# Newton results kept in PSUM, and the first norm and first weights prepared without GpSimd

## The chip, the cores and the metric

The kernel runs on one core of a Trainium2 chip. The time is device time in microseconds (us) of one launch. Before the change it is 2960.99 us, the median of three runs (2956.82 to 2964.68). The profile is of one further execution, which took 2968.41 us.

Names: PE is TensorE's matmul queue, PEld its weight loads, DVE is VectorE, ACT is ScalarE, POOL is GpSimd, SP is SyncE, which issues all DMAs here.

## The reference, cut to what matters

The kernel computes one layer of a hybrid encoder for 1280 tokens (1024 and 256) of width 1024: an RMS norm, one wide input projection, three mixers (latent attention, a bidirectional RWKV-7 scan, cross-attention to memory tokens), gates, an output projection, and a gated convolution MLP. The change touches the first part alone, the projections and the norms in them:

```python
h = rms_norm(x, norm_mix_g);  proj = h @ w_in            # c_q, c_kv, k_r, rw, xq, gates
q = rms_norm(rms_norm(c_q, q_norm_g) @ w_uq, mla_qn_g)   # per head of 96, then rope
k = rms_norm(concat(rms_norm(c_kv) @ w_ukv, k_r), mla_kn_g)
kk = k7 * k_k;  kk = kk / max(sqrt(sum(kk * kk)), 1e-12) # per head of 64
m = rms_norm(mem) @ w_mkv;  xqh = rms_norm(xq, x_qn_g);  mk = rms_norm(mk, x_kn_g)
```

Every `rms_norm` over channels is a sum of squares and one over its root.

## The kernel before, in words

Activations stand transposed: channels on the 128 partitions, tokens along the row, in three chunks of 512, 512 and 256 tokens (`CH`). Every matmul is done in three passes, because each fp32 operand is split into a high part `h` and a rest `l` (`split`, line 123: the copy that rounds on ACT or DVE, and the subtraction on POOL or DVE); the passes are lines 133, 134 and 135 in `mm3`.

The norm of the input is not applied before the projection. `norm1` (line 392) loads a chunk of x, multiplies by the gain and splits it into `hh` and `hl` (`scaled_split`, lines 284 and 285), sums the squares of its eight channel tiles into `nacc` (`mean_sq`, lines 272 to 279, where squares and additions take turns on ACT, DVE and POOL), and leaves a generator, `norm1_stats`, that splits `nacc`, sums it over the partitions with two matmuls against ones (`col_sum`, line 239, into a PSUM tile `nst` with the tag `tr`), and makes one over the root. That is `rsq`: on ACT the logarithm, the exponential and its square (lines 251 to 253), then on DVE one step of Newton in two instructions (lines 256 and 257). The result, `rbc`, is scaled once more (line 263), and every projection is multiplied by it when it leaves PSUM, as in line 424 for `xq` and 879 for the gates; a q head leaves through lines 679 and 680.

Four PSUM banks with the tag `mm` hold projections, four with the tag `tr` hold the small sums and transposes. A projection's bank comes free when DVE or ACT has read it.

Order of the work. `xq_proj` (line 436) comes first: it loads the weights `wqf` in eight pieces and splits them (line 446), and goes through chunk 0 channel tile by channel tile for all four heads at once, so that PE can start when the first tile is there. In that loop, at `k == 6`, `drain` runs what is left of the norm, `col_sum` included, so that its two matmuls stand in PE's queue between tiles 5 and 6. All four `mm` banks are then full, and chunk 1 can't start before line 424 has emptied one. Chunks 1 and 2 follow, then the memory's projection, gates, latents, q heads (`q_out`), keys (`k_out`), values and the RWKV tiles (`rw_out`), interleaved by generators. Weights of 128 columns come through `w4_load` (line 315), two tiles in flight, in the order of `w4_order`; `xq_proj` calls it once ahead of chunks 1 and 2.

The order on each engine's queue is fixed at compile time: a planner takes the instructions by priority (the order of the program, unless a block asks for high priority) as soon as its own simulated clock says that they are ready. On the chip each queue is then worked off in that order.

Of the kernel before, what the change touches and what calls it, by code (L numbers as in the profile page):

```python
# [11 lines left out]
ALU = mybir.AluOpType  # L12
# [15 lines left out]
EPS = 1e-6  # L28
# [69 lines left out]
class Kern:  # L98
# [128 lines left out]
    def parts(self, p, x, cn, K=128):  # L227

        hi = p.tile([128, 512], F32R, tag="sqh", name="sqh", bufs=2)
        lo = p.tile([128, 512], F32R, tag="sql", name="sql", bufs=2)  # L230
        self.split(x[:K, :cn], hi[:K, :cn], lo[:K, :cn])
        return hi, lo
# [14 lines left out]
    def rsq(self, y, t, tmp, scale=1.0, eps=0.0):  # L247


        nc = self.nc  # L250
# [4 lines left out]
        s, op, c = (eps / scale, ALU.add, -3.0 / scale) if eps else (-0.5 * scale, ALU.mult, 1.5)  # L255
        nc.vector.scalar_tensor_tensor(out=tmp, in0=t, scalar=s, in1=tmp, op0=op, op1=ALU.mult)
# [11 lines left out]
    def mean_sq(self, p, src, cn):  # L268
# [4 lines left out]
        for k in range(1, 8):  # L273
            sq = p.tile([128, 512], F32, tag="nsq", name="nsq", bufs=3)
            if k % 2:
# [3 lines left out]
            (nc.vector if k % 2 else nc.gpsimd).tensor_add(out=acc[:, :cn], in0=acc[:, :cn], in1=sq[:, :cn])  # L279
# [112 lines left out]
    def norm1(self, p, ci, w=None):  # L392
# [16 lines left out]
        acc = self.mean_sq(p, lambda k: x[k], cn)  # L409
# [4 lines left out]
    def norm1_stats(self, p, acc, ci):  # L414
        c0, cn = CH[ci]
        x = self.parts(p, acc, cn)
        yield
        yield from self.rsq_x(p, self.rbc1[ci], x, cn)

    def head_norm(self, p, ps, cn, rbc, gain, dst):  # L420
# [9 lines left out]
        yield from self.rsq(sq[:, :cn], self.col_sum(x, cn), tmp[:, :cn], 1.0 / 128, EPS)  # L430
        nc.vector.scalar_tensor_tensor(
            out=raw[:, :cn], in0=raw[:, :cn], scalar=gain, in1=sq[:, :cn], op0=ALU.mult, op1=ALU.mult
# [3 lines left out]
    def xq_proj(self, p):  # L436
# [4 lines left out]
        def load(k):  # L441
# [4 lines left out]
            self.split(f, wq[0][:, k, :], wq[1][:, k, :], "dve")  # L446
# [8 lines left out]
        for k in range(8):  # L455
            if k == 6:
# [12 lines left out]
        self.w4_load()  # L469
        for ci in (1, 2):  # L470
            c0, cn = CH[ci]
            for h in range(4):
# [197 lines left out]
    def q_out(self, p, ps, h, c0, cn):  # L670
# [16 lines left out]
        yield from self.rsq(sq[0:96, :cn], st[0:96], zs[0:96, :cn], EPS / 384)  # L687
        nc.vector.tensor_mul(out=z[0:96, :cn], in0=z[0:96, :cn], in1=sq[0:96, :cn])
# [34 lines left out]
    def k_out(self, p, ps, j, kro, c0, cn):  # L723
# [13 lines left out]
        yield from self.rsq(sq[:, :cn], st, tmp[:, :cn])  # L737
        nc.vector.tensor_mul(out=z[:, :cn], in0=z[:, :cn], in1=sq[:, :cn])
        i = (3 * j + c0 // 512) % 2
        for e in range(2):  # L740
            kr = self.krb[64 * e : 64 * e + 32, 512 * i : 512 * i + 512]
            (nc.vector if e else nc.gpsimd).tensor_mul(out=kr[:, :cn], in0=kro[:, cs], in1=sq[64 * e : 64 * e + 32, :cn])
# [57 lines left out]
    def rw_out(self, p, m, x, g2):  # L800
# [7 lines left out]
        elif m < 8:  # L808
# [4 lines left out]
            for c0, cn in CH:  # L813
# [8 lines left out]
                yield from self.rsq(sq[:, :cn], st, tmp[:, :cn])  # L822
                nc.vector.scalar_tensor_tensor(
                    out=kk[:, c0 : c0 + cn], in0=xc, scalar=self.vec("k_k", j), in1=sq[:, :cn],
# [1276 lines left out]
```

## Time and profile before

| | us |
|---|---|
| median of three runs | 2960.99 |
| profiled execution, its own time | 2968.41 |
| its span | 2966.6 |
| PE busy in the span | 2781.4 (94%) |
| DVE, ACT, POOL busy | 1544.2, 1173.3, 1358.5 |
| chain that ended last: share of PE | 38% |

Stages by time: `xq` up to about 92 us, memory and gates to about 120, latents and q heads to about 372, keys and values to about 516, RWKV tiles to about 640; the scan with attention as its filler to about 1950, and after that the output projection and the MLP, in which PE is busy nearly without a break. [...]

### The profile page before, as it was taken

The page shows a single profiled execution, that of the slowest core. Times are in us where ns is not written, and L with a number is a line of the kernel's source. Part 1 is how long each engine was busy: PE and PEld are TensorE (multiplying, and loading weights), DVE is VectorE, ACT ScalarE, POOL GpSimd, SP SyncE. Part 2 cuts the span into 40 slices and gives each one's busy share as a digit, 9 for nine tenths or more (in the row PEclk, how much of TensorE's full clock was granted, in tenths as well). Part 3 has the DMA queues.
Part 4 walks back from the last instruction along what each step waited for, and adds up shares of the span by engine and source line. Part 5 has one row for each costly group of instructions (what it writes and reads, how often), then busy time and mean ns, then how long its engine had stood idle before and what let it go on. Part 6 is the DMA issues. An engine that isn't in the chain of part 4 may idle for free. (4 is left out here: it accounts for less than half of the span.)

```text
span 2966.6 us, 50241 instructions
## 1 busy us (share of the span) xinstructions
PE 2781.4 (94%) x19556; PEld 2246.2 (76%) x19556; DVE 1544.2 (52%) x2576; ACT 1173.3 (40%) x2561; POOL 1358.5 (46%) x1220
## 2 busy tenths in 40 slices
PE   7998998999999999899989688999999999999999
PEld 5787787885666665477767577888888888888888
DVE  8638848566767665655565465423422323323233
ACT  5645555545555555544443234423221211212111
POOL 5546736454444344455554467743342332423323
PEclk8999999999999998899989899999999999999999
DMA  4333324553122222343343666422111111111112
GB/s 151 99 96 97 101 69 114 154 147 90 51 68 61 59 60 78 89 122 108 106 122 102 189 201 187 144 87 64 40 43 36 42 37 36 43 36 42 37 33 86
DMA packets 250005, 261.77 MB, mean 88 GB/s; under 512 B 81028, under 2 KB 178448, under 8 KB 249768
## 3 DMA queue, kind: packets, MB, share of 16 engines
q1 hardware_dynamic: 249768, 258.57, 29.6%
q8 instruction: 154, 2.52, 0.4%
q14 instruction: 83, 0.68, 0.1%
HBM read 196.64 MB, written 61.73 MB: 87 GB/s over the span
## 5 line engine op out<-in xcount | busy, mean ns | idle before, releaser
L133 PE MATMUL up<-h2h,wuh 128*128 128x512 f32 (+1 forms) x1056 | 374.2, 354 | 0.0
L134 PE MATMUL up<-h2h,wul 128*128 128x512 f32 (+1 forms) x1056 | 374.0, 354 | 0.0
L135 PE MATMUL up<-h2l,wuh 128*128 128x512 f32 (+1 forms) x1056 | 373.5, 354 | 0.0
L129 POOL TENSOR_TENSOR w4l<-w4f,w4h 128x512 fp32r<-128x512 f32 (+1 forms) x154 | 264.0, 1723 | 216.5 <-ACT w4h L126 210.4
L129 POOL TENSOR_TENSOR wul<-wuf,wuh 128x1024 fp32r<-128x1024 f32 x52 | 125.1, 2405 | 270.7 <-ACT wuh L126 270.7
L133 PEld LDWEIGHTS up<-h2h,wuh 128*128 128x128 f32 x1056 | 199.7, 189 | 28.0
L135 PEld LDWEIGHTS up<-h2l,wuh 128*128 128x128 f32 x1056 | 199.6, 189 | 27.8
L134 PEld LDWEIGHTS up<-h2h,wul 128*128 128x128 f32 x1056 | 199.7, 189 | 27.4
L1849 DVE TENSOR_TENSOR x<-x,dn 128x512 f32<-128x512 f32 (+1 forms) x192 | 113.6, 598 | 194.3 <-PE dn L135 194.3
L133 PE MATMUL proj<-hh,w4h 128*128 128x512 f32 (+1 forms) x504 | 182.2, 363 | 9.3 <-DVE go L879 5.0
L134 PE MATMUL dn<-ah,wdl 128*128 128x256 f32 (+1 forms) x528 | 187.2, 356 | 0.0
L135 PE MATMUL dn<-al,wdh 128*128 128x256 f32 (+1 forms) x528 | 184.7, 356 | 0.0
L133 PE MATMUL dn<-ah,wdh 128*128 128x256 f32 (+1 forms) x528 | 182.1, 356 | 0.4 <-ACT wdh L126 0.4
L135 PE MATMUL proj<-hl,w4h 128*128 128x512 f32 (+1 forms) x504 | 181.4, 360 | 0.0
L134 PE MATMUL proj<-hh,w4l 128*128 128x512 f32 (+1 forms) x504 | 181.0, 360 | 0.0
L126 ACT CAST w4h<-w4f 128x512 fp32r<-128x512 f32 (+1 forms) x154 | 113.2, 751 | 149.6 <-DMA w4f<-in_w_g 41.1
L133 PE MATMUL gt<-ghh,w4h 128*128 128x512 f32 x384 | 163.7, 426 | 8.3 <-ACT w4h L126 5.2
L126 ACT CAST wuh<-wuf 128x1024 fp32r<-128x1024 f32 x52 | 54.7, 1052 | 291.7 <-PE up L135 276.1
L1869 DVE TENSOR_TENSOR fraw<-up,rbc 128x512 f32<-128x512 f32 (+1 forms) x66 | 39.8, 604 | 247.7 <-PE up L135 241.0
L129 POOL TENSOR_TENSOR wdl<-wdf,wdh 128x384 fp32r<-128x384 f32 (+1 forms) x64 | 60.3, 944 | 225.1 <-ACT wdh L126 225.1
L937 DVE TENSOR_REDUCE m<-mx 128x1 f32<-128x512 f32 (+1 forms) x184 | 107.6, 601 | 105.7 <-PE mx L936 105.1
L134 PE MATMUL gt<-ghh,w4l 128*128 128x512 f32 x384 | 155.5, 405 | 7.3 <-POOL w4l L129 7.3
(392 smaller groups left out, 7418.3 us busy)
## 6 DMA issues: line engine op xcount, KB each, us to landing
w4f<-in_w_g SPq DMA_DIRECT2D x48, 512.0 KB
wuf<-in_w_up SPq DMA_DIRECT2D x44, 512.0 KB
rk<-s_rk SPq DMA_DIRECT2D x80, 192.0 KB
w4f<-in_w_g SPq DMA_DIRECT2D x48, 256.0 KB
s_gT<-go SPq DMA_DIRECT2D x40, 256.0 KB
mg<-s_gT SPq DMA_DIRECT2D x40, 256.0 KB
wdf<-in_w_down SPq DMA_DIRECT2D x48, 192.0 KB
w4f<-in_w_rw SPq DMA_DIRECT2D x30, 256.0 KB
```

What stands on the lines that cost most here:

```text
L126: nc.scalar.copy(out=hi, in_=x)
L129: (nc.gpsimd if el == "pool" else nc.vector).tensor_sub(out=lo, in0=x, in1=hi.bitcast(F32))
L133: mm(ps, lhsT=lh, rhs=rh, start=first, stop=False)
L134: mm(ps, lhsT=ll, rhs=rh, start=False, stop=False)
L135: mm(ps, lhsT=lh, rhs=rl, start=False, stop=last)
L937: nc.vector.tensor_reduce(out=m2[:, n, z : z + 1], in_=ps[:, :kn], axis=AX.X, op=ALU.max)
L1849: nc.vector.tensor_add(out=xc, in0=xc, in1=ps[:, :cn])
L1869: nc.vector.tensor_mul(out=raw[:, o : o + cn], in0=ps, in1=self.rbc[:, c0 : c0 + cn])
```

## The change

Four things change.

1. `rsq` takes an `out`. With it, both DVE instructions of the Newton step write to the bank that holds the sums, and what uses the result reads it from there. `head_norm`, `q_out`, `k_out` and the `kk` part of `rw_out` do so; the norms of x, of the memory and of the latents don't.
2. In `k_out` the rope part of the key is multiplied on DVE for both heads; before, one of the two was on POOL.
3. The first norm and the first weights: the weights `wqf` are rounded on ACT and subtracted on DVE (before: DVE and POOL); `mean_sq` for x has all squares on ACT and all additions on DVE; the split of `nacc` subtracts on DVE; that split and the whole of `rsq_x` have high priority in the planner.
4. The `drain` in chunk 0 comes at `k == 7`, and the first `w4_load` between chunks 1 and 2.

```diff
@@ -224,11 +224,11 @@
         n = x.shape[1]
         self.nc.gpsimd.tensor_tensor(out=out, in0=x, in1=self.mhalf.to_broadcast([128, n]), op=ALU.pow)
 
-    def parts(self, p, x, cn, K=128):
+    def parts(self, p, x, cn, K=128, el="pool"):
 
         hi = p.tile([128, 512], F32R, tag="sqh", name="sqh", bufs=2)
         lo = p.tile([128, 512], F32R, tag="sql", name="sql", bufs=2)
-        self.split(x[:K, :cn], hi[:K, :cn], lo[:K, :cn])
+        self.split(x[:K, :cn], hi[:K, :cn], lo[:K, :cn], "act", el)
         return hi, lo
 
     def col_sum(self, parts, cn, K=128, ones=None):
@@ -244,7 +244,7 @@
         with self.tc.issue_after(after.ins):
             self.nc.scalar.preload_act_table_set("natural_log_exp_and_others")
 
-    def rsq(self, y, t, tmp, scale=1.0, eps=0.0):
+    def rsq(self, y, t, tmp, scale=1.0, eps=0.0, out=None):
 
 
         nc = self.nc
@@ -253,6 +253,10 @@
         self.last = nc.scalar.activation(out=tmp, in_=y, func=AF.Square)
         yield
         s, op, c = (eps / scale, ALU.add, -3.0 / scale) if eps else (-0.5 * scale, ALU.mult, 1.5)
+        if out is not None:
+            nc.vector.scalar_tensor_tensor(out=out, in0=t, scalar=s, in1=tmp, op0=op, op1=ALU.mult)
+            nc.vector.scalar_tensor_tensor(out=out, in0=out, scalar=c, in1=y, op0=ALU.add, op1=ALU.mult)
+            return
         nc.vector.scalar_tensor_tensor(out=tmp, in0=t, scalar=s, in1=tmp, op0=op, op1=ALU.mult)
         nc.vector.scalar_tensor_tensor(out=y, in0=tmp, scalar=c, in1=y, op0=ALU.add, op1=ALU.mult)
 
@@ -265,18 +269,18 @@
     def small(self, p, n, tag):
         return p.tile([128, n], F32, tag=f"{tag}{n}", name=tag, bufs=2)
 
-    def mean_sq(self, p, src, cn):
+    def mean_sq(self, p, src, cn, alone=False):
 
         nc = self.nc
         acc = p.tile([128, 512], F32, tag="nacc", name="nacc", bufs=3)
         nc.scalar.activation(out=acc[:, :cn], in_=src(0), func=AF.Square)
         for k in range(1, 8):
             sq = p.tile([128, 512], F32, tag="nsq", name="nsq", bufs=3)
-            if k % 2:
+            if k % 2 or alone:
                 nc.scalar.activation(out=sq[:, :cn], in_=src(k), func=AF.Square)
             else:
                 nc.vector.tensor_mul(out=sq[:, :cn], in0=src(k), in1=src(k))
-            (nc.vector if k % 2 else nc.gpsimd).tensor_add(out=acc[:, :cn], in0=acc[:, :cn], in1=sq[:, :cn])
+            (nc.vector if k % 2 or alone else nc.gpsimd).tensor_add(out=acc[:, :cn], in0=acc[:, :cn], in1=sq[:, :cn])
         return acc
 
     def scaled_split(self, x, g, hi, lo):
@@ -406,16 +410,19 @@
                 w(k + z)
         for k in range(8):
             self.scaled_split(x[k], self.vec("g_mix", k), hh[:, k, :], hl[:, k, :])
-        acc = self.mean_sq(p, lambda k: x[k], cn)
+        acc = self.mean_sq(p, lambda k: x[k], cn, True)
         job = self.norm1_stats(p, acc, ci)
         self.jobs.append(job)
         self.step(job)
 
     def norm1_stats(self, p, acc, ci):
         c0, cn = CH[ci]
-        x = self.parts(p, acc, cn)
+        with self.tc.high_priority():
+            x = self.parts(p, acc, cn, el="dve")
         yield
-        yield from self.rsq_x(p, self.rbc1[ci], x, cn)
+        with self.tc.high_priority():
+            for _ in self.rsq_x(p, self.rbc1[ci], x, cn):
+                pass
 
     def head_norm(self, p, ps, cn, rbc, gain, dst):
 
@@ -427,9 +434,10 @@
         x = self.parts(p, sq, cn)
         yield
         tmp = p.tile([128, 512], F32, tag="tmp", name="tmp", bufs=2)
-        yield from self.rsq(sq[:, :cn], self.col_sum(x, cn), tmp[:, :cn], 1.0 / 128, EPS)
+        st = self.col_sum(x, cn)
+        yield from self.rsq(sq[:, :cn], st, tmp[:, :cn], 1.0 / 128, EPS, st)
         nc.vector.scalar_tensor_tensor(
-            out=raw[:, :cn], in0=raw[:, :cn], scalar=gain, in1=sq[:, :cn], op0=ALU.mult, op1=ALU.mult
+            out=raw[:, :cn], in0=raw[:, :cn], scalar=gain, in1=st, op0=ALU.mult, op1=ALU.mult
         )
         nc.sync.dma_start(out=dst, in_=raw[:, :cn])
 
@@ -443,7 +451,7 @@
             nc.sync.dma_start(
                 out=f.rearrange("p (m c) -> p m c", c=128), in_=io["w_tok"][6:10, :, k, :].rearrange("m p c -> p m c")
             )
-            self.split(f, wq[0][:, k, :], wq[1][:, k, :], "dve")
+            self.split(f, wq[0][:, k, :], wq[1][:, k, :], "act", "dve")
 
         def tile_of(h):
             return [x[:, :, h * 128 : (h + 1) * 128] for x in wq]
@@ -453,7 +461,7 @@
         nc.sync.dma_start(out=self.ident, in_=io["ident"])
         ps = [self.pp.tile([128, 512], F32, tag="mm", name="proj") for h in range(4)]
         for k in range(8):
-            if k == 6:
+            if k == 7:
                 self.drain()
                 after = self.last
             for h in range(4):
@@ -466,9 +474,10 @@
         with self.tc.issue_after(after.ins):
             self.norm1(p, 2)
         self.drain()
-        self.w4_load()
         for ci in (1, 2):
             c0, cn = CH[ci]
+            if ci == 2:
+                self.w4_load()
             for h in range(4):
                 ps = self.pp.tile([128, 512], F32, tag="mm", name="proj")
                 self.gemm(tile_of(h), self.h[ci], 8, ps[:, :cn])
@@ -684,8 +693,8 @@
         nc.vector.scalar_tensor_tensor(
             out=st, in0=st, scalar=4.0 / EPS, in1=self.fb[:, c0 : c0 + cn], op0=ALU.mult, op1=ALU.add
         )
-        yield from self.rsq(sq[0:96, :cn], st[0:96], zs[0:96, :cn], EPS / 384)
-        nc.vector.tensor_mul(out=z[0:96, :cn], in0=z[0:96, :cn], in1=sq[0:96, :cn])
+        yield from self.rsq(sq[0:96, :cn], st[0:96], zs[0:96, :cn], EPS / 384, out=st[0:96])
+        nc.vector.tensor_mul(out=z[0:96, :cn], in0=z[0:96, :cn], in1=st[0:96])
         nc.sync.dma_start(out=io["qT"][h][:, c0 : c0 + cn], in_=z[0:96, :cn])
 
     def k_rope(self, p):
@@ -734,12 +743,12 @@
             out=st, in0=st, scalar=1.0 / 96, in1=self.fb[:, cs], op0=ALU.mult, op1=ALU.add
         )
         tmp = p.tile([128, 512], F32, tag="qzs", name="tmp", bufs=2)
-        yield from self.rsq(sq[:, :cn], st, tmp[:, :cn])
-        nc.vector.tensor_mul(out=z[:, :cn], in0=z[:, :cn], in1=sq[:, :cn])
+        yield from self.rsq(sq[:, :cn], st, tmp[:, :cn], out=st)
+        nc.vector.tensor_mul(out=z[:, :cn], in0=z[:, :cn], in1=st)
         i = (3 * j + c0 // 512) % 2
         for e in range(2):
             kr = self.krb[64 * e : 64 * e + 32, 512 * i : 512 * i + 512]
-            (nc.vector if e else nc.gpsimd).tensor_mul(out=kr[:, :cn], in0=kro[:, cs], in1=sq[64 * e : 64 * e + 32, :cn])
+            nc.vector.tensor_mul(out=kr[:, :cn], in0=kro[:, cs], in1=st[64 * e : 64 * e + 32])
             nc.sync.dma_start(out=io["kaT"][2 * j + e][0:64, cs], in_=z[64 * e : 64 * e + 64, :cn])
             nc.sync.dma_start(out=io["kaT"][2 * j + e][64:96, cs], in_=kr[:, :cn])
 
@@ -819,9 +828,9 @@
                 st = self.col_sum(y, cn, ones=self.blkr)
                 nc.vector.tensor_scalar(out=st, in0=st, scalar1=1e-24, scalar2=None, op0=ALU.max)
                 tmp = p.tile([128, 512], F32, tag="qzs", name="tmp", bufs=2)
-                yield from self.rsq(sq[:, :cn], st, tmp[:, :cn])
+                yield from self.rsq(sq[:, :cn], st, tmp[:, :cn], out=st)
                 nc.vector.scalar_tensor_tensor(
-                    out=kk[:, c0 : c0 + cn], in0=xc, scalar=self.vec("k_k", j), in1=sq[:, :cn],
+                    out=kk[:, c0 : c0 + cn], in0=xc, scalar=self.vec("k_k", j), in1=st,
                     op0=ALU.mult, op1=ALU.mult,
                 )
             for e in range(2):
```

## Rows read from the trace of the kernel before

**Rows 1.** windows: span us, busy us of each engine (instructions), granted clock, DMA share, GB/s

```profile
0.00:35.00 35.00, 21.66 (x74) 15.16 (x74) 29.29 (x44) 19.41 (x31) 18.77 (x15) 0.94 0.72 230
35.00:92.00 57.00, 46.47 (x215) 37.26 (x216) 47.84 (x65) 33.39 (x65) 32.20 (x23) 0.89 0.24 78
92.00:120.00 28.00, 24.31 (x139) 20.55 (x139) 20.33 (x28) 19.00 (x40) 14.55 (x12) 1.00 0.28 92
...
250.00:372.00 122.00, 107.05 (x542) 90.01 (x541) 105.16 (x143) 63.99 (x124) 82.59 (x72) 0.95 0.34 100
...
455.00:516.00 61.00, 49.56 (x298) 43.38 (x297) 54.13 (x65) 31.86 (x65) 41.41 (x38) 0.94 0.44 118
```

**Rows 2.** timeline of PE: start, us, what; in brackets idle before and its releaser

```profile
29.86 0.50 PE L239 MATMUL nst<-sqh,onesr 128*128 128x512 f32 x1 [1.94 <-ACT sqh L126]
33.27 0.80 PE L239 MATMUL nst<-sql,onesr 128*128 128x512 f32 x1 [2.92 <-POOL sql L129]
35.48 2.07 PE L133 MATMUL proj<-hh,xqh 128*128 128x512 f32 x4 [1.41 <-DVE xqh L128]
...
51.98 0.80 PE L133 MATMUL proj<-hh,xqh 128*128 128x512 f32 x1 [6.14 <-DVE raw L424]
```

**Rows 3.** timeline of DVE, 18 to 56 us

```profile
22.17 0.74 DVE L285 SCALAR_TENSOR_TENSOR hl<-x,vt,hh 128x512 fp32r<-128x512 f32 x1
...
23.84 1.75 DVE L279 TENSOR_TENSOR nacc<-nacc,nsq 128x512 f32<-128x512 f32 x1
...
35.02 0.41 DVE L128 CAST xqh<-wqf 128x512 fp32r<-128x512 f32 x1
35.35 0.68 DVE L279 TENSOR_TENSOR nacc<-nacc,nsq 128x512 f32<-128x512 f32 x1
...
42.45 0.68 DVE L256 SCALAR_TENSOR_TENSOR tmp<-nst,tmp 128x512 f32<-128x512 f32 x1
...
47.26 1.48 DVE L263 TENSOR_SCALAR rbc<-rbc 128x512 f32<-128x512 f32 x1
48.66 2.67 DVE L285 SCALAR_TENSOR_TENSOR hl<-x,vt,hh 128x256 fp32r<-128x256 f32 x4
51.25 1.27 DVE L424 TENSOR_TENSOR raw<-proj,rbc 128x512 f32<-128x512 f32 x2
```

**Rows 4.** timeline of POOL, 18 to 56 us

```profile
23.33 1.71 POOL L129 TENSOR_TENSOR xql<-wqf,xqh 128x512 fp32r<-128x512 f32 x1 [1.63 <-DVE xqh L128]
```

**Rows 5.** groups of ACT by form, 0 to 60 us: count, busy us, mean ns, idle before

```profile
L284 ACT ACTIVATE hh<-x,vt 128x512 fp32r<-128x512 f32 x16 | 11.0, 717 | 5.6 <-DMA x<-in_xT 5.6
L276 ACT ACTIVATE nsq<-x 128x512 f32<-128x512 f32 x8 | 5.0, 623 | 8.8 <-POOL nacc L279 5.1 <-DVE nacc L279 3.7
...
L126 ACT CAST sqh<-nacc 128x512 fp32r<-128x512 f32 x2 | 1.2, 616 | 0.0
```

**Rows 6.** waits of PE, 250 to 372 us: total, times, longest

```profile
PE q L133 <- DVE qzs L680: 6.2, 5, 2.6
```

**Rows 7.** groups of DVE by form, 0 to 700 us

```profile
L688 DVE TENSOR_TENSOR qz<-qz,nsq 96x512 f32<-96x512 f32 x16 | 19.5, 1218 | 0.3
L257 DVE SCALAR_TENSOR_TENSOR nsq<-qzs,nsq 96x512 f32<-96x512 f32 x16 | 17.9, 1116 | 0.3
...
L742 DVE TENSOR_TENSOR krb<-kro,nsq 32x512 f32<-32x512 f32 x8 | 12.6, 1572 | 0.2
...
L684 DVE SCALAR_TENSOR_TENSOR nst<-nst,fb 128x512 f32<-128x512 f32 x16 | 11.0, 690 | 2.9 <-PE nst L239 2.8
...
L256 DVE SCALAR_TENSOR_TENSOR qzs<-nst,qzs 96x512 f32<-96x512 f32 x16 | 10.9, 682 | 3.8 <-ACT qzs L253 3.7
...
L688 DVE TENSOR_TENSOR qz<-qz,nsq 96x256 f32<-96x256 f32 x8 | 8.5, 1067 | 0.2
...
L256 DVE SCALAR_TENSOR_TENSOR qzs<-nst,qzs 96x256 f32<-96x256 f32 x8 | 3.3, 415 | 0.1
```

**Rows 8.** instructions that waited for line 688: total us, times

```profile
  ACT nsq L675: 25.9, 13
```

## The prediction

> **What bounds the kernel now.** I read the page's busy shares first: PE is busy 94% of the span, so only PE's idle time and its low clock can be won, and a change to other engines counts where PE waits for them. The table of windows then says where that is in the part that the change touches. In [rows 1] PE is idle for 35.00 - 21.66 = 13.3 us of the first stretch (5.4 of them before the first matmul), 10.5 us of 35 to 92, 3.7 of 92 to 120, 15.0 of 250 to 372 and 11.4 of 455 to 516. The stretches between them have almost none and are not shown. The same rows give the granted clock: 0.89 in 35 to 92, 0.95 in 250 to 372. A stretch of 57 us at 0.89 does 6.3 us less work than at full clock; one of 122 us at 0.95, 6.1 less; one of 61 us at 0.94, 3.7 less. The low clock stands behind the pauses, so it falls with them.
>
> Next, what ends each wait. At the start it is the first norm [rows 2]: PE stands before the sums' first half (1.94 us, for ACT), before the second (2.92, for POOL), before tile 6 (1.41, for the weight's rounding on DVE), and before chunk 1 (6.14, until line 424 empties a bank). Chunk 1 begins at 51.98. The chain of that norm is long because of DVE's queue [rows 3]: the sums are there at 34.1, line 256 runs at 42.45, line 263 at 47.26, then four splits of chunk 2 go ahead for 2.67 us, and line 424 starts at 51.25. In the same rows an addition takes 1.75 us once and 0.68 another time, with the same shape. POOL splits weights beside the long one, for 1.71 us from 23.33 [rows 4]. DVE is busy 29.3 of 35 us and 47.8 of 57 [rows 1].
>
> From 250 to 372 PE mostly waits for a projection's bank to be read by DVE, 6.2 us for line 680 alone [rows 6], and DVE is busy 105 of 122 us [rows 1]. Of DVE's work there, the groups by form show two kinds [rows 7]. With one operand in PSUM (lines 256, 684) the 512 columns take 0.682 and 0.690 us. With both in SBUF (257, 688) they take 1.116 and 1.218 on average. Line 688 also holds ACT up: 25.9 us of ACT's idle time end with it [rows 8], since the next square reuses the buffer that line 688 reads last.
>
> **The change part by part.**
>
> *Newton's results in PSUM.* Line 256 now writes PSUM from PSUM and SBUF, and 257 and its reader have one operand in PSUM. That form is on the trace: line 684 reads and writes the same bank at 0.690 [rows 7]. So I take 0.69 for 512 columns and 0.415 for 256. For the q heads: 16 x (1.218 - 0.69) = 8.4 us and 8 x (1.067 - 0.415) = 5.2 at line 688, 16 x (1.116 - 0.69) = 6.8 at line 257; 20.4 us of DVE's time without the 256-wide forms of line 257, nearly all of it in 250 to 372. DVE then falls from 105 to about 85 us there, from 86% to 70%. The buffer that ACT waits for is free one instruction earlier (1.218 us in the mean). Bounds for PE: nothing, if the waits are re-ended by something else; all 15.0 of idle time and 6.1 of clock, if they vanish. I take half of the idle time, 7.5, and half of the clock's loss, 3: 10 us.
>
> [...]
>
> *Keys.* From 455 to 516 DVE is busy 54 of 61 us [rows 1]. The rope product of line 742 takes 1.572 on DVE [rows 7] and becomes 0.69 with its operand in PSUM; 12 more of them come over from POOL, so 8 x 0.88 = 7.0 are saved and 8 x 0.69 + 4 x 0.415 = 7.2 added: nothing in sum. What is left is the same saving as above on line 257 and its readers, less per instruction. With 11.4 us idle and 3.7 of clock at stake, bounds are 0 and 15 (and a loss of 7 if the 12 added products cost what they do now with two SBUF operands); I take 5, the third.
>
> *The first norm.* ACT gets 8 roundings of the weights and 3 squares more for chunk 0. In all it then has 8 x (0.717 + 0.623 + 0.616) = 15.6 us [rows 5] for chunk 0, from 4 us on: done at 20 us. DVE has 8 x (0.74 + 0.68 + 0.68) = 16.8 [rows 3], the subtraction by the addition's row, from 5: done at 22, if POOL is still. The rest of the norm, at high priority, is a rounding, a subtraction, two sums, three ACT steps, three on DVE and line 424, eleven steps of 0.4 to 0.7: 6 us, and about 2 for hand-overs: 30 us. PE has by then 24 matmuls of tiles 6 and 7 to do after 27.9 (the start of the wait that ends at 29.86 [rows 2]); at the stretch's mean of 21.66 / 74 = 0.29 us they end at 34.9. So PE and not the norm decides when chunk 1 begins: 35 at the earliest, 17 us sooner than now. Against that, the splits of chunk 1 (8 x 0.74 = 5.9 us) may be planned ahead of line 424, as four of chunk 2 are now [rows 3]. I put chunk 1 at 38: 14 us. The clock: 0.89 over 57 us costs 6.3, and the pause of 6.14 us is one of its causes; I take 2. Bounds: 0, if DVE's or ACT's backlog gives it back before 120 us, and 17 + 6 + 3.7 = 27.
>
> Here ACT is what hides the cost, and it is near its limit: 19.4 + 33.4 + 19.0 = 71.8 us of 120 before [rows 1], plus 8 roundings (4.9) and nine squares that were DVE's (5.0) makes 82 of about 104 if 16 are won. It is late next, then DVE.
>
> *The moved w4_load and drain.* Two loads of 256 KB, two roundings and two subtractions on POOL come later. Nothing in them waits for other work, so the planner can put them where SP is idle; chunk 2's matmuls on the four heads hide them. If the cover is gone, the first gate waits for one rounding and one POOL split, 0.6 + 1.7 us [rows 4, 5]. On SP's queue the loads of x for chunk 1 come that much sooner. The drain's move is in the 14 us above. I count nothing for either, at worst -3.
>
> **Sum.** 16 + 10 + 5 = 31 us. The profiled execution took 2968.4, of which 2966.6 are the span, so it goes to 2937. It stands 7.4 above the median of the runs; the stages ahead of 516 us can't be compared run by run, so I take the same 31 from 2961: **2930**. The later stages, from 700 us on, start earlier and otherwise stay; PE's long busy end has nothing that these edits could shorten.
>
> **Rivals.**
>
> *The start gives its gain back.* ACT or the weight loads of gates and memory become the bound between 60 and 120 us. For it: ACT's 82 us above. Against it: PE idles only 3.7 us in 92 to 120. Only the 15 of the later parts remain: 2946.
>
> *The q heads and keys don't move.* PE's waits there end with DVE, but DVE itself may wait for a store or for ACT. For it: half of its groups of line 688 could be hidden anyway. Against it: DVE at 86 to 89% [rows 1]. Only 16: 2945.
>
> *Neither holds*, or the planner, whose clock is not the chip's, lays the queues so that new waits eat what is won. Or the instructions stay long although they read PSUM. 2957, no change that can be measured; I call less than 0.3%, 9 us, that.
>
> *Slower: the sums' banks.* The bank `nst` is now held until the last reader, two instructions longer. PE takes its queue in order, so a `col_sum` without a bank stops all projections. A q chunk comes every 122 / 24 = 5.1 us, and four `tr` banks last 20 us; it decides from there. The chain from the first sum to line 688 is about 12 us: two halves of the sum apart by a POOL split, then seven steps on two busy engines. Against it stands that distance; for it, that the RWKV tiles take such banks at the same time. If every chunk waited for the two instructions more, 24 x (1.116 + 1.218) = 56 us [rows 7] would be lost; with a rotation that waits at about half of them, 28, and 7 for the added products, against 16 from the start: 2980.
>
> **How the numbers follow.** Forecast 0.54 (its own range 2912 to 2944), start given back 0.15, q and keys unmoved 0.15, neither 0.09, banks 0.07. The two partial rivals lie 15 us under the time before and are faster for the most part; of each I give 0.02 to no change. Faster by over 0.3%: 0.54 + 0.13 + 0.13 - 0.01 = 0.79; within: 0.13; slower: 0.08. The range: all bounds together, 27 + 21 + 15 = 63 below, 2898, is too much to come at once; I end it at 2906, and above at 2955, which takes in both partial rivals and leaves out the last two.
>
> **What would show it.** Right: chunk 1's first matmul at 35 to 40 us; no POOL instruction among the splits of the weights and the sums of x; lines 257 and 688 at 0.69 for 512 columns; DVE about 20 us less busy through the q heads, and PE's waits for lines 680 and 879 halved. Wrong: line 424 still behind splits, with chunk 1 near 45 or later; PE waiting for ACT at 60 to 120 us by more than now; `col_sum` released by line 688 or 738, which is the banks' rival; or PSUM forms that take over 0.8 us. If the time after 700 us changes by more than a few us, the planner has changed something that this sum doesn't hold.

## The result, and the profile after

| | before | after |
|---|---|---|
| median, us | 2961.29 (4 runs, 2956.82 to 2964.68) | 2922.35 (4 runs, 2916.70 to 2924.39) |
| profiled execution, its own time | 2968.41 | 2923.37 |
| its span | 2966.6 | 2921.5 |

The ratio is 0.987, with a 95% interval of 0.9851 to 0.9888: 39 us or 1.3% faster. Forecast were 31 us and 2930, in a range of 2906 to 2955.

The same windows of the kernel after, as in [rows 1] (span, busy us of PE, weight loads, DVE, ACT and POOL with their instructions, granted clock, DMA share, GB/s). The work has moved forward, so that a window holds somewhat later work than before:

```profile
0.00:35.00 35.00, 26.16 (x98) 20.29 (x98) 29.73 (x57) 29.64 (x54) 3.64 (x6) 1.00 0.87 275
35.00:92.00 57.00, 51.38 (x278) 43.41 (x279) 46.27 (x78) 42.59 (x84) 23.25 (x17) 0.94 0.22 74
92.00:120.00 28.00, 27.61 (x122) 22.11 (x121) 9.20 (x19) 16.28 (x33) 18.52 (x16) 1.00 0.40 124
...
250.00:372.00 122.00, 116.78 (x608) 96.63 (x607) 80.19 (x129) 67.59 (x128) 72.55 (x68) 0.99 0.33 98
...
455.00:516.00 61.00, 58.63 (x379) 53.00 (x379) 45.95 (x75) 38.05 (x73) 28.82 (x30) 1.00 0.54 147
```

PE is idle for 8.8 us of the first window in place of 13.3, for 5.6 in place of 10.5 of the second, 0.4 in place of 3.7 of the third, 5.2 in place of 15.0 of the fourth and 2.4 in place of 11.4 of the fifth, and the granted clock is at 0.94 to 1.00 where it was 0.89 to 0.95 in all but the third. POOL has 3.6 us of work in the first 35 where it had 18.8, and ACT 29.6 where it had 19.4. DVE, at 105 of 122 us in the fourth, is at 80, but part of this is later work that has moved in. The same work, from PE's first matmul of the q heads to its first of the keys, compares as follows, first before, then after:

```profile
214.10:429.30 215.20, 200.25 (x1019) 167.12 (x1018) 155.25 (x207) 114.88 (x210) 123.06 (x111) 0.97 0.31 93
```

```profile
197.90:399.40 201.50, 195.88 (x1018) 163.22 (x1017) 130.89 (x207) 113.59 (x210) 118.87 (x111) 0.99 0.33 99
```

The same 207 instructions take DVE 24.4 us less. PE's idle time falls from 15.0 to 5.6 us, and its matmuls take 4.4 us less at the higher clock, 0.99 in place of 0.97: 13.7 us in sum.

PE's own timeline of the start after (start, us, what; in brackets the idle time before and what ended it), against [rows 2]:

```profile
26.09 0.40 PE L239 MATMUL nst<-sqh,onesr 128*128 128x512 f32 x1
...
27.25 0.40 PE L239 MATMUL nst<-sql,onesr 128*128 128x512 f32 x1
...
38.29 0.79 PE L239 MATMUL nst<-sqh,onesr 128*128 128x512 f32 x1 [4.79 <-ACT sqh L126]
39.22 0.80 PE L133 MATMUL proj<-hh,xqh 128*128 128x512 f32 x1
```

The sums of the first norm no longer stop PE. Chunk 1 begins at 39.22 in place of 51.98. Ahead of it PE still stands for 4.79 us, now for the sums of chunk 1's norm, which wait for a rounding on ACT. ACT's timeline shows why that is late:

```profile
32.48 3.29 ACT L288 ACTIVATE hh<-x,vt 128x256 fp32r<-128x256 f32 x8
...
37.62 0.61 ACT L126 CAST sqh<-nacc 128x512 fp32r<-128x512 f32 x1
```

DVE had added up chunk 1's squares at 33.5; ACT first took the eight roundings of chunk 2 and some squares.

DVE's timeline of the same kernel, against [rows 3]:

```profile
28.94 1.78 DVE L283 TENSOR_TENSOR nacc<-nacc,nsq 128x512 f32<-128x512 f32 x1
...
33.44 0.68 DVE L260 SCALAR_TENSOR_TENSOR tmp<-nst,tmp 128x512 f32<-128x512 f32 x1
...
36.62 0.42 DVE L267 TENSOR_SCALAR rbc<-rbc 128x512 f32<-128x512 f32 x1
36.95 1.27 DVE L289 SCALAR_TENSOR_TENSOR hl<-x,vt,hh 128x256 fp32r<-128x256 f32 x3
...
38.48 2.48 DVE L431 TENSOR_TENSOR raw<-proj,rbc 128x512 f32<-128x512 f32 x4
```

From the norm's first Newton instruction to the line that empties the banks (424 before, 431 now) it takes 5.0 us where it took 8.8. Three splits of chunk 2 still stand between the last step and that line. It empties its first bank at about 39.1, so PE could not have begun chunk 1 before that without the sums either.

The groups by form on DVE after (count, busy us, mean ns, idle before), against [rows 7]; 258 is the second Newton instruction, 697 its reader in the q heads (688 before), 751 the keys' rope product (742):

```profile
L257 DVE SCALAR_TENSOR_TENSOR nst<-nst,qzs 96x512 f32<-96x512 f32 x16 | 11.0, 689 | 4.6 <-ACT qzs L253 4.5
L258 DVE SCALAR_TENSOR_TENSOR nst<-nst,nsq 96x512 f32<-96x512 f32 x16 | 11.0, 688 | 0.2
...
L697 DVE TENSOR_TENSOR qz<-qz,nst 96x512 f32<-96x512 f32 x16 | 10.9, 680 | 0.4
L751 DVE TENSOR_TENSOR krb<-kro,nst 32x512 f32<-32x512 f32 x16 | 10.8, 677 | 0.2
```

All of them take 0.68 to 0.69 us, as the form with one operand in PSUM did before (0.682 and 0.690). How it came about is in the extremes of one line, first before, then after (count, then shortest, median and longest in ns; the shortest are of 256 columns):

```profile
L688 DVE TENSOR_TENSOR qz<-qz,nsq x24: 421/1006/3606, 229.8 to 368.0; 96x512 f32<-96x512 f32 x16, 96x256 f32<-96x256 f32 x8
```

```profile
L697 DVE TENSOR_TENSOR qz<-qz,nst x24: 405/674/685, 214.1 to 340.0; 96x512 f32<-96x512 f32 x16, 96x256 f32<-96x256 f32 x8
```

Before, half of the executions of line 688 took 1.0 us or more, up to 3.6; after, none is over 685 ns. What runs beside the long ones is POOL, as here (from the timelines of DVE and POOL before):

```profile
282.35 1.20 POOL L129 TENSOR_TENSOR sql<-nsq,sqh 96x256 fp32r<-96x256 f32 x1
282.99 3.61 DVE L688 TENSOR_TENSOR qz<-qz,nsq 96x512 f32<-96x512 f32 x1
283.52 2.53 POOL L129 TENSOR_TENSOR w4l<-w4f,w4h 128x512 fp32r<-128x512 f32 x2
```

Of the 32 executions of lines 257 and 688 with 512 columns in the q heads before, the 13 that have no POOL instruction beside them take 0.67 to 0.69 us; the 16 that take 0.77 or more all have one. After, most of the 32 have POOL beside them too, and none takes over 0.70.

PE's waits in the q heads (total us, times, longest):

```profile
PE nst L239 <- POOL sql L129: 3.1, 2, 2.9
PE proj L133 <- DVE qzs L689: 1.8, 3, 0.7
```

PE had waited 6.8 us for line 680 (6.2 of them in [rows 6]); for the same line, 689 now, it waits 2.1 (1.8 of them above).

Where the time comes from is read best by when a stage begins, from the traces of all kernels. Each column is PE's first matmul of a stage, in us: the memory's projection, the q heads, the keys, the first scores of the attention, the scan.

| kernel | median | memory | q | keys | scores | scan |
|---|---|---|---|---|---|---|
| before | 2961 | 102.3 | 214.1 | 429.3 | 639.9 | 681.3 |
| after | 2922.4 | 86.9 | 197.9 | 399.4 | 598.8 | 638.9 |
| start alone | 2944.7 | 87.8 | 199.3 | 414.9 | 626.4 | 667.8 |
| PSUM results alone | 2931.7 | 98.7 | 213.1 | 413.9 | 612.3 | 652.0 |
| POOL back in the start | 2933.2 | 99.2 | 212.1 | 413.1 | 610.9 | 651.5 |
| no priority | 2918.3 | 87.2 | 199.1 | 399.0 | 598.8 | 638.1 |
| first Newton step only | 2930.8 | 87.3 | 199.0 | 405.1 | 613.2 | 655.0 |
| keys as before | 2934.0 | 86.9 | 198.8 | 402.3 | 612.8 | 652.1 |
| chunk 2 behind | 2920.8 | 89.7 | 201.0 | 402.4 | 600.5 | 640.7 |
| weights only | 2922.3 | 94.4 | 206.0 | 407.0 | 605.1 | 644.8 |
| rope products on DVE | 2943.8 | 88.0 | 199.5 | 416.2 | 627.0 | 670.1 |
| three banks | 2921.2 | 87.4 | 200.2 | 400.0 | 598.3 | 641.4 |
| drain and load as before | 2915.3 | 87.0 | 197.7 | 398.3 | 595.5 | 635.5 |
| two more banks | 2926.1 | 89.7 | 206.3 | 406.7 | 604.8 | 645.0 |

From before to after the gain is 15.4 us at the memory's projection, 16.2 at the q heads, 29.9 at the keys, 41.1 at the scores and 42.4 at the scan. What follows the scan's start differs from one trace to the next: to the first down projection of the MLP it is 1423.1 us before and 1420.4 after, 1408.8 with the start alone and 1415.6 with drain and load as before, though no edit touches it; one trace of each kernel can't tell whether that is the kernel or the execution. Runs of one kernel spread over 5 to 21 us, and the interval of a ratio reaches 5 to 9 us to either side. So medians of two changed kernels that are under some 10 us apart settle little, and for the stages ahead of the scan the table says more, though it has one execution of each.

### The profile page after: what moved, and what is told of

Same layout as the page of the kernel before. It is cut to its first block, busy times and chain, and to the rows that moved or that the text cites. A ratio compares the mean times of both kernels' runs of the same rounds, so it can differ in the third digit from the quotient of the medians.

```text
span 2921.5 us, 50264 instructions
## 1 busy us (share of the span) xinstructions
PE 2766.6 (95%) x19556; PEld 2237.2 (77%) x19556; DVE 1481.6 (51%) x2591; ACT 1176.7 (40%) x2578; POOL 1301.6 (45%) x1188
## 4 chain that ended last, share of the span: by engine, by line
PE 53%; DVE 6%; DMA 4%; issue 2%; ACT 2%; POOL 1%; SPq 1%; DVEq 0%; ACTq 0%; POOLq 0%
PE up L133 7%; PE up L134 7%; PE up L135 7%; PE dn L133 4%; PE dn L134 3%; PE dn L135 3%; PE gt L133 2%; PE gt L134 2%; PE gt L135 2%; PE ao L1090 1%; PE wo_ps L133 1%; PE wo_ps L134 1%; PE wo_ps L135 1%; DMA mg<-s_gT 1%; PE st L133 1%
## 5 line engine op out<-in xcount | busy, mean ns | idle before, releaser
L1090 PE MATMUL ao<-pf,va 128*65 128x512 f32 (+1 forms) x288 | 147.4, 594 | 15.6 <-ACT os L1094 15.5
```

Source lines behind the costliest of these rows:

```text
L1090: nc.tensor.matmul(ot[0][out, :cn], lhsT=lhsT, rhs=rhs, start=start, stop=stop)
```

## Experiments

**The start alone.** The changed kernel with all Newton results back in SBUF and the rope products on both engines:

```diff
-        yield from self.rsq(sq[:, :cn], st, tmp[:, :cn], 1.0 / 128, EPS, st)
+        yield from self.rsq(sq[:, :cn], self.col_sum(x, cn), tmp[:, :cn], 1.0 / 128, EPS)
...
-            nc.vector.tensor_mul(out=kr[:, :cn], in0=kro[:, cs], in1=st[64 * e : 64 * e + 32])
+            (nc.vector if e else nc.gpsimd).tensor_mul(out=kr[:, :cn], in0=kro[:, cs], in1=sq[64 * e : 64 * e + 32, :cn])
```

> The kernel before with parts 3 and 4 of the change alone (first norm and first weights without GpSimd, high priority, drain and w4_load moved); every Newton result stays in SBUF and the rope product of the keys on both engines. My theory: the start and the PSUM results add up, so this keeps the 15 to 16 us by which the memory's first matmul came earlier (86.9 against 102.3) and wins nothing later: 2945 us, 0.5% under before, and the q heads wait for DVE as they did. Rival, the start's gain is given back once DVE is congested in the q heads: 2957 to 2961, with the first q matmul early and the first key matmul at its old place.

Measured: 2944.7, ratio 0.9942 (0.9923 to 0.996), 16 us. The memory starts at 87.8, the q heads 14.8 earlier than before, the keys 14.4 earlier. The start's gain is kept, and nothing is won in the q heads.

**The PSUM results alone.** The other half:

```diff
-            self.split(f, wq[0][:, k, :], wq[1][:, k, :], "act", "dve")
+            self.split(f, wq[0][:, k, :], wq[1][:, k, :], "dve")
...
-        acc = self.mean_sq(p, lambda k: x[k], cn, True)
+        acc = self.mean_sq(p, lambda k: x[k], cn)
```

(also without the priority, and with the drain and w4_load in their old places)

> The kernel before with parts 1 and 2 alone (Newton results in PSUM, rope product of the keys on DVE). My theory: 22 to 28 us faster, 2933 to 2939, from the q heads (14) and the keys and values (13), with chunk 1's first matmul at 45 to 52 us as before; together with the start alone the two gains make the whole 39. Rival, the start needs this part too because the head norms shorten DVE's queue there: then this one gives more than 28, and the start alone less than 10.

Measured: 2931.7, ratio 0.9902 (0.9881 to 0.9922), 29 us. Chunk 1 starts at 51.83 as before; 3.6 us are won by the memory's projection, of which 1.0 is left at the q heads, 14.4 more between q heads and keys, and 29.3 in all by the scan. The sum of the two halves is 16 + 29 = 45 against 39 for the whole, the difference within what the medians resolve; in the traces at the scan it is 13.5 + 29.3 = 42.8 against 42.4. The halves add up.

**POOL back in the start.** The engines of the first weights, of the sums of squares and of the norm's split as before, the order as changed:

```diff
-            self.split(f, wq[0][:, k, :], wq[1][:, k, :], "act", "dve")
+            self.split(f, wq[0][:, k, :], wq[1][:, k, :], "dve")
...
-        acc = self.mean_sq(p, lambda k: x[k], cn, True)
+        acc = self.mean_sq(p, lambda k: x[k], cn)
...
-            x = self.parts(p, acc, cn, el="dve")
+            x = self.parts(p, acc, cn)
```

> The changed kernel with the first weights, the sums of squares and the split of the first norm back on the engines of before (DVE and POOL), but with high priority, the drain at tile 7 and the later w4_load kept. My theory, by which contention with POOL and POOL's slow subtractions made the first norm late: 8 to 12 us slower than the changed kernel, 2930 to 2934. Rival, it is the order (priority and drain) that brings the gain: within 3 us of the changed kernel, 2922 to 2925.

Measured: 2933.2, 11 us above the changed kernel; ratio to before 0.9901 (0.9882 to 0.992). The whole start is as it was, though priority, drain and load are changed. PE's timeline:

```profile
29.67 0.51 PE L239 MATMUL nst<-sqh,onesr 128*128 128x512 f32 x1 [1.94 <-ACT sqh L126]
33.09 0.79 PE L239 MATMUL nst<-sql,onesr 128*128 128x512 f32 x1 [2.92 <-POOL sql L129]
```

and its wait ahead of chunk 1 (total us, times, longest):

```profile
PE proj L133 <- DVE raw L431: 6.1, 1, 6.1
```

These are the waits of [rows 2], to less than 0.1 us each and 0.2 us sooner. So the gain of the start comes from the exchange of engines. Whether it is because POOL's own steps are slow (1.71 us for a subtraction that DVE does in 0.7), or because they stretch DVE's instructions beside them (1.75 us for an addition that takes 0.68 another time, [rows 3]), these runs don't separate; the traces show both.

**No priority.** The same question from the other side:

```diff
-        with self.tc.high_priority():
-            x = self.parts(p, acc, cn, el="dve")
+        x = self.parts(p, acc, cn, el="dve")
...
-        with self.tc.high_priority():
-            for _ in self.rsq_x(p, self.rbc1[ci], x, cn):
-                pass
+        yield from self.rsq_x(p, self.rbc1[ci], x, cn)
```

> The changed kernel without the two high-priority blocks in norm1_stats; the engines stay as changed. My theory: 3 to 5 us slower than the changed kernel, since splits of chunk 1 and 2 go ahead of the norm's steps on DVE and ACT: 2925 to 2927. Rival, order is what counts: 10 us or more slower, 2932 and up.

Measured: 2918.3, ratio 0.9851 (0.9831 to 0.9872). The stages start within 1.2 us of the changed kernel's. Both theories expected a loss; there is none. With these engines the priority does nothing that can be seen.

**Drain and load as before.**

```diff
-            if k == 7:
+            if k == 6:
                 self.drain()
...
+        self.w4_load()
         for ci in (1, 2):
             c0, cn = CH[ci]
-            if ci == 2:
-                self.w4_load()
```

> The changed kernel with the drain back at tile 6 and w4_load back ahead of chunks 1 and 2; engines and priority as changed. My theory: the norm is ready in time now and the planner puts the loads where SP is idle, so neither place counts: within 2 us of the changed kernel, 2920 to 2925, chunk 1's first matmul within 1 us of 39.2. Rival, the sums stand in PE's queue too early and PE waits for them: chunk 1 at 42 or later, 2926 and up.

Measured: 2915.3 (2908.4 to 2925.1), ratio 0.9836 (0.9811 to 0.986): the fastest median of all and below the 2920 to 2925 that I expected, but its interval overlaps that of the changed kernel. Chunk 1 begins at 39.30. At the scan it is 3.4 us ahead. So part 4 of the change wins nothing, and may cost some 3 us; no run here shows why.

**Weights only.** Of the start's engines, only the weights as changed:

```diff
-        acc = self.mean_sq(p, lambda k: x[k], cn, True)
+        acc = self.mean_sq(p, lambda k: x[k], cn)
...
-            x = self.parts(p, acc, cn, el="dve")
+            x = self.parts(p, acc, cn)
```

> The changed kernel with the first weights on ACT and DVE as changed, but the squares, their sums and the norm's split on DVE and POOL as before. My theory: the weights are the larger half, because POOL's eight subtractions of 1.7 us go and with them most of the contention: 3 to 6 us slower than the changed kernel, chunk 1's first matmul at 43 to 46 us: 2925 to 2928. Rival, the sums' chain through POOL is what counts: chunk 1 at 49 or later and 9 us or more slower, 2931 and up.

Measured: 2922.3, the changed kernel's median, ratio 0.9866 (0.9841 to 0.9891). The trace says more than the median: chunk 1 at 46.95, the memory's projection at 94.4, 7.9 of the 15.4 us won, and 5.9 us behind the changed kernel at the scan. That the later stages made this up in the timed runs isn't explained by anything in the edit. With POOL back it had been 99.2 at the memory's projection and 651.5 at the scan, so the weights bring 4.8 of the 12.3 us that the engines bring at the one place, and 6.7 of 12.6 at the other: about half, not the larger half that I expected, and chunk 1 came later than the 43 to 46 of my theory.

**First Newton step only.**

```diff
-            nc.vector.scalar_tensor_tensor(out=out, in0=out, scalar=c, in1=y, op0=ALU.add, op1=ALU.mult)
+            nc.vector.scalar_tensor_tensor(out=y, in0=out, scalar=c, in1=y, op0=ALU.add, op1=ALU.mult)
```

(and the readers take `sq` again)

> The changed kernel, but only the first of the two Newton instructions writes PSUM; the second reads it and writes the result to SBUF, as before, and its readers have two SBUF operands again (the keys' rope product on both engines). My theory, by which what counts is how many of DVE's instructions escape POOL: about half of the PSUM part is lost, since the second Newton instruction stays short (0.69 for 512 columns) and line 697 goes back to 1.0 to 1.2: 12 to 16 us slower than the changed kernel, 2935 to 2939. Rival, the gain comes from the sums' buffer in SBUF, which ACT's next square gets one instruction earlier: then nearly all of it is lost, as the buffer is held to the last reader again: 2943 to 2946.

Measured: 2930.8, 8 us above the changed kernel; ratio 0.9883 (0.9854 to 0.9912). Through the q heads it wins 9.1 of the 13.7 us (from q to keys 206.1, against 215.2 before and 201.5 after). Its groups on DVE:

```profile
L697 DVE TENSOR_TENSOR qz<-qz,nsq 96x512 f32<-96x512 f32 x16 | 19.9, 1244 | 0.6
...
L258 DVE SCALAR_TENSOR_TENSOR nsq<-nst,nsq 96x512 f32<-96x512 f32 x16 | 10.9, 682 | 0.4
```

and who waited for line 697:

```profile
  ACT nsq L684: 25.5, 12
```

ACT waits for the sums' buffer as long as in [rows 8], and yet two thirds of the q heads' gain is there: these 9.1 us come from the time of DVE's instructions and not from the buffer. Of the other 4.6 this run can't tell line 697's time from the buffer, since it gives up both.

Behind the q heads nearly everything is lost: from the keys to the scan it takes 249.9 us, against 252.0 before and 239.5 after. At the scan this kernel is 16.1 us behind the changed one, where I expected 12 to 16; the 8 us between the medians are less, and their intervals overlap.

**Keys as before.**

```diff
-        yield from self.rsq(sq[:, :cn], st, tmp[:, :cn], out=st)
-        nc.vector.tensor_mul(out=z[:, :cn], in0=z[:, :cn], in1=st)
+        yield from self.rsq(sq[:, :cn], st, tmp[:, :cn])
+        nc.vector.tensor_mul(out=z[:, :cn], in0=z[:, :cn], in1=sq[:, :cn])
...
-            nc.vector.tensor_mul(out=kr[:, :cn], in0=kro[:, cs], in1=st[64 * e : 64 * e + 32])
+            (nc.vector if e else nc.gpsimd).tensor_mul(out=kr[:, :cn], in0=kro[:, cs], in1=sq[64 * e : 64 * e + 32, :cn])
```

> The changed kernel with the keys (k_out) as before: result in SBUF, rope products on DVE and POOL. It asks for the term that I sized too small (keys and values: 5 forecast, about 13 in the traces). My theory: the keys alone carry 6 to 10 us, 2928 to 2932, and POOL's and DVE's rope products of 1.6 us come back. Rival, the gain there comes from the kk tiles and the freer buffers: under 3 us slower, 2922 to 2925.

Measured: 2934.0, 12 us above the changed kernel; ratio 0.9898 (0.9871 to 0.9925). From the keys to the scan it takes 249.8 us, against 239.5 after and 252.0 before: the keys carry 10.3 of the 12.5 us. The medians say the same, though their intervals just overlap. PE's waits from keys to values, first in this kernel, then in the changed one (total us, times, longest):

```profile
PE proj L133 <- DVE go L888: 3.2, 1, 3.2
PE k L133 <- DVE go L888: 2.2, 1, 2.2
PE nst L239 <- ACT sqh L126: 1.9, 1, 1.9
PE v L135 <- POOL uwl L129: 1.5, 1, 1.5
```

```profile
PE gt L133 <- DVE rraw L779: 0.9, 1, 0.9
PE proj L133 <- DVE rraw L779: 0.8, 1, 0.8
PE nst L239 <- ACT vso L848: 0.8, 1, 0.8
PE k L133 <- DVE go L888: 0.7, 2, 0.4
```

**Rope products on DVE.** The start alone, and of the rest only this:

```diff
-            (nc.vector if e else nc.gpsimd).tensor_mul(out=kr[:, :cn], in0=kro[:, cs], in1=sq[64 * e : 64 * e + 32, :cn])
+            nc.vector.tensor_mul(out=kr[:, :cn], in0=kro[:, cs], in1=sq[64 * e : 64 * e + 32, :cn])
```

> The kernel with the start alone changed (2944.7) and, of the rest, one thing: both rope products of the keys are on DVE, with both operands in SBUF; no result is in PSUM. My theory, the operand in PSUM is what shortens DVE and the twelve products more cost DVE 1.2 us each: no gain, 0 to 6 us slower than the start alone, 2945 to 2951, with PE's waits for DVE in the keys as before. Rival, POOL rid of its twelve products of 1.6 us is what won the 11 us of the keys: 2934 to 2938.

Measured: 2943.8, ratio 0.9935 (0.9915 to 0.9954), the same as the start alone; the keys begin at 416.2 and the scan at 670.1. Without its twelve products on POOL, the kernel wins nothing. The products on DVE, in the start alone and here:

```profile
L750 DVE TENSOR_TENSOR krb<-kro,nsq 32x512 f32<-32x512 f32 x8 | 12.6, 1570 | 0.2
...
L750 DVE TENSOR_TENSOR krb<-kro,nsq 32x256 f32<-32x256 f32 x4 | 5.0, 1253 | 0.1
```

```profile
L750 DVE TENSOR_TENSOR krb<-kro,nsq 32x512 f32<-32x512 f32 x16 | 14.5, 906 | 0.2
...
L750 DVE TENSOR_TENSOR krb<-kro,nsq 32x256 f32<-32x256 f32 x8 | 4.3, 535 | 0.1
```

24 products take 18.8 us where 12 took 17.6. The price of 1.2 us for each one added was wrong: with POOL's twin gone, each is shorter.

**Three banks.**

```diff
-self.pool("psT", space=PSUM, bufs=4) as pt
+self.pool("psT", space=PSUM, bufs=3) as pt
```

> The changed kernel with three PSUM banks for the small sums in place of four. It asks how near the longer hold of the sums' bank comes to a wait. My theory: a bank is held some 10 us and one is asked for every 4.5 us in the q heads, so three are just enough: 0 to 5 us slower than the changed kernel, 2922 to 2927. The prediction's rival, the banks are nearly used up by the longer hold: sums released by the last readers of the banks, 10 us or more slower, 2932 and up.

Measured: 2921.2, ratio 0.9863 (0.9839 to 0.9886), no change; the scan starts at 641.4 against 638.9. Even three banks hold out, so the rival of the prediction that ended on the slower side had no ground here.

**Chunk 2 behind, and two more banks.** Two tries at the 4.8 us that are left at the start, both without the priority. The first queues DVE's splits of chunk 2 behind the emptying of the banks, the second puts two heads of chunk 1 into banks of the small sums:

```diff
-        with self.tc.issue_after(after.ins):
+        with self.tc.issue_after(after.ins), self.tc.issue_after(self.raw.ins):
             self.norm1(p, 2)
```

```diff
+                sums = ci == 1 and h < 2
-                ps = self.pp.tile([128, 512], F32, tag="mm", name="proj")
+                ps = (self.pt if sums else self.pp).tile([128, 512], F32, tag="tr" if sums else "mm", name="proj")
```

> The changed kernel without the high priority, and with DVE's splits of chunk 2 queued behind the last line that empties a bank of chunk 0 (today eight of them stand between the norm's steps and that line). My theory, DVE's order is what delays chunk 1: its first matmul at 35 to 36 us in place of 39.2, 3 to 4 us faster than the kernel without priority: 2914 to 2916. Rival, chunk 2's splits are then late and PE waits for them at 60 us: 2918 to 2922.

> The kernel without the high priority, and the first two heads of chunk 1 written to two banks of the small sums, so that PE need not wait for chunk 0's banks to be emptied (4.8 us idle at 33.5 now, and a low clock after it). My theory: chunk 1's first matmul at 33.5 to 35, and 3 to 6 us won up to the memory's projection (its first matmul at 81 to 84), 2913 to 2917. Rival, ACT and DVE are the bound of the start by then and give it back before the memory's projection, whose first matmul stays at 86 to 88: 2917 to 2922.

Measured for the first: 2920.8, ratio 0.9852 (0.9826 to 0.9879). DVE empties the banks at 35.60 and PE begins chunk 1 at 36.35, 2.9 us sooner; no sum stands ahead of it now, the next comes at 42.05. DVE's timeline shows what is late instead, eight splits of chunk 2 that now take 6.43 us:

```profile
35.07 0.43 DVE L267 TENSOR_SCALAR rbc<-rbc 128x512 f32<-128x512 f32 x1
35.60 2.48 DVE L428 TENSOR_TENSOR raw<-proj,rbc 128x512 f32<-128x512 f32 x4
38.00 6.43 DVE L289 SCALAR_TENSOR_TENSOR hl<-x,vt,hh 128x256 fp32r<-128x256 f32 x8
```

Further on PE waits once more for a bank, in chunk 2, which it does nowhere between chunk 1 and the gates in the changed kernel. Line 428, which empties that bank, had itself waited, for a store (first PE, then DVE):

```profile
70.22 0.58 PE L133 MATMUL proj<-hh,xqh 128*128 128x256 f32 x1 [2.80 <-DVE raw L428]
```

```profile
69.48 1.41 DVE L428 TENSOR_TENSOR raw<-proj,rbc 128x512 f32<-128x512 f32 x2 [2.72 <-DMA s_xqT<-raw]
```

The memory's projection starts at 89.7, 2.8 us later than in the changed kernel. What is won at 36 us is gone at 90. The late splits of chunk 2, which my rival named, end no wait of PE that the profile shows; what the store waited for was not followed up.

Measured for the second: 2926.1, ratio 0.9873 (0.9848 to 0.9898). Chunk 1 begins at 39.13, 0.5 us earlier than without priority alone (39.66):

```profile
38.20 0.79 PE L239 MATMUL nst<-sqh,onesr 128*128 128x512 f32 x1 [4.78 <-ACT sqh L126]
```

PE stood for the sums of chunk 1's norm, which are ahead of chunk 1's matmuls in its queue and wait for ACT's rounding. The row had said so in the profile after; the forecast failed at reading it. The banks come free at nearly the same time: without priority PE waits 0.18 us more for line 428 when the sums' matmul is done. So neither step alone could win more than some 1 us. The q heads begin 7.2 us later than without priority; why was not followed up.

## Why the prediction was right, and where it was not

**The direction and the sum.** 31 us were forecast, 39 measured by the medians, 42.4 at the start of the scan. By the traces the terms are 16.2 for the start (16 forecast), 13.7 for the q heads (10) and 12.5 from the keys on (5).

**The first norm: the number right, half of its reasons wrong.** Chunk 1 was put at 38 and came at 39.2; a loss of the gain before 120 us didn't come, since PE is idle 0.4 us in 92 to 120. But I counted on the high priority for the norm's steps, and on the drain. Without the priority nothing is lost; with POOL back, priority and drain win nothing. The start's gain is all from the exchange of engines. The chain itself ran as worked out only in its first part: the sums were done at 27.7, and line 431 ran at 38.5 and not at 30, with splits of chunk 2, an addition stretched to 1.78 us beside POOL's splits, and additions for chunk 1 ahead. So it was the norm and not PE that decided when chunk 1 began: PE was done with chunk 0 at 33.5 and stood for 4.8 us. The 3 us that I had allowed for splits of chunk 1 ahead of line 424 happened to cover what stood there instead; that the number fits is in part luck. ACT as the next bound did show, but at another place: that wait of 4.8 us ends with ACT's rounding. Between 60 and 120, where I had looked for it, PE waits 1.7 us for ACT, against 3.1 before, and the gain is not given back.

**Results in PSUM: right, sized somewhat too small.** From the q heads to the keys DVE is busy 24.4 us less (20.4 forecast, without the shorter forms of line 257), and the forms cost 0.68 to 0.69. I took half of PE's idle time for safety, 7.5 us; 9.3 of 15.0 went, and 4.4 us of PE's busy time with the clock, where I had taken 3. The run with only the first Newton step shows that the buffer, which I had offered as a second cause, is not needed for 9.1 of the 13.7 us; for the rest it stays open.

Lines 688 and 697 are the same product, with two operands in SBUF before and with one after: the longest execution took 3606 ns before and 685 after. That operand in PSUM has no price that these instructions show: the 512 columns of line 697 take 680 ns in the mean, and those executions of lines 257 and 688 before that had no POOL instruction beside them 0.67 to 0.69 us.

**Keys: the step that was mis-sized.** It was the sentence by which the moved rope products cost as much as the PSUM operand saves, "nothing in sum", and the third of the stakes that I took for the rest. Measured are 10 to 12 us for the keys. The products cost 14.1 us in all, where DVE alone spent 16.4 before, and POOL's 16.4 went. The sum had left out what DVE's four products of 256 columns save, 0.94 us each before and 0.41 after. It had also not seen that the product on POOL stretches the one on DVE beside it, 1.57 us in the mean with it and 0.91 without.

Three runs leave this on the keys. Moving the products alone wins nothing. Leaving all of the keys in SBUF loses 10.3 of the 12.5 us. And with the first Newton result in PSUM but the last one in SBUF, 10.4 of them are lost too, although both Newton instructions then have an operand in PSUM. So it is the last result in PSUM, for the instructions that read it, that carries the keys; which of these readers carries most was not tried. The buffer is not excluded as a cause here: ACT's next square waits for the rope products 8.0 us in the kernel with the keys as before, 12.0 with the products on DVE and 13.8 with the first Newton step only, and in the changed kernel not at all.

**The rivals.** The start kept its gain, the q heads and keys moved, and with four banks for the sums, or three, no loss by their longer hold can be seen.

## What to carry to other kernels

Where DVE's instructions of one shape have two lengths, look at how many operands they have in SBUF and what POOL does beside them; with an intermediate kept in the PSUM bank that it came from, the instructions here went from means of 1.12 and 1.22 us to 0.68 and 0.69, the length that the form with two operands in SBUF had with nothing of POOL's beside it (0.67 to 0.69). The gain of such an edit is not the sum of the shorter instructions but the waits of the bound engine that end with them: 24.4 us less of DVE's work in the q heads took 9.3 us of PE's idle time, and 4.4 us of the clock's loss went with it. And before working on a stall, read which instruction stands first in the queue of the engine that waits: an earlier buffer helped little here while a sum was ahead that waited for another engine (two more banks: 0.5 us).

## What was not expected of the hardware

POOL's instructions of one shape differ in length as well. In the q heads of the changed kernel fifteen of sixteen subtractions of 96x512 take 1.28 to 1.30 us, and one takes 3.60:

```profile
256.40 1.29 POOL L129 TENSOR_TENSOR sql<-nsq,sqh 96x512 fp32r<-96x512 f32 x1
...
266.71 3.60 POOL L129 TENSOR_TENSOR sql<-nsq,sqh 96x512 fp32r<-96x512 f32 x1
```

Beside the long one DVE runs an instruction with two SBUF operands of 1281 columns:

```profile
267.65 1.54 DVE L791 SCALAR_TENSOR_TENSOR rx<-rraw,vt,rx 128x1281 f32<-128x1281 f32 x1
```

That instruction's 1.54 us don't cover the 2.3 by which the subtraction is longer; what makes up the rest is open. PE stands 2.92 us for that subtraction, the longest wait left in the q heads. And 24 products on one engine took hardly longer than 12 with 12 more on POOL beside them (18.8 against 17.6 us).
